# Scores of both query halves in one run of narrow products

## Chip, cores and metric

The kernel runs on one core of a Trainium2 chip. Its time is the device time of one execution in microseconds (us). The core has TensorE for matrix products (PE in profiles, its weight loads PEld), VectorE (DVE), ScalarE (ACT), GpSimd (POOL) and SyncE (SP), which issues the DMAs. Each engine works through its own queue in a fixed order; a semaphore makes an instruction wait for another engine. TensorE writes its sums into PSUM: eight banks, each of 128 rows by 512 float32 columns. VectorE and ScalarE read them from there.

## What is computed

Two layers of a decoder trunk over 256 positions of width 1024: a gated feed-forward half-step, a mixer, a second half-step and a gated embedding. Inside the mixer three branches run on one input projection `u @ w_in`. The change touches the first branch, in which an indexer chooses for each query the 64 keys that it may attend to:

```python
q_pos = j * Q_BLOCK + jnp.arange(Q_BLOCK)            # Q_BLOCK = 128: two halves
causal = key_pos[None, :] <= q_pos[:, None]
idx = jnp.einsum("bqh,bqhs->bqs", wi,
                 jax.nn.relu(jnp.einsum("bqhd,bsd->bqhs", qi, k_idx)))
idx = jnp.where(causal[None], idx.astype(jnp.float32), -jnp.inf)
_, sel = lax.top_k(idx, k_top)                       # k_top = 64
```

The other branches are a pooling mixer and a state-space mixer (SSD) with a causal depthwise convolution of width 4, `silu(causal_depthwise_conv(xbc, conv_w, conv_b))`, and a factor `silu(z)`.

## The kernel before

**Wide products.** Each float32 product is made of three products of rounded parts (`mm3`, L208 to L213): high by high, high by low, low by high. A column tile of a projection (128 output columns, 256 positions) is 24 such products of 128x256 over eight slices of the input. Weights come in units of 128x1024: SyncE loads `raw`, ScalarE rounds it to `whi` (L145), VectorE makes the remainder `wlo` (L146), with five buffers of each. One unit feeds 24 products.

**Banks.** All eight banks belong to one pool with two tags of four buffers (`bank`, L97): `mm` for wide products, two column tiles to a bank, and `aux` for everything else. A bank is taken again when its readers are done with it.

**The woven stage.** In the mixer three generators take turns by a plan of due times (`weave`): `choose` (key norms, transposes, then the indexer of the first and of the second half), `silus` (six pairs of column tiles for the convolution, four pairs of `z`, two of `q`) and `gates`. A pair of the convolution's input is read from its bank column tile by column tile: ScalarE scales it (L771), VectorE adds three shifted taps (L773, shapes 128x255, 128x254, 128x253), ScalarE takes the silu (L776). A gate pair is read by one tanh (L632), a `z` pair by one silu (L618).

**The indexer.** A narrow product multiplies 64 rows instead of 128; two of them, on the upper and the lower rows of the array, write two banks in turn (`products`). The first half of the queries sees 128 keys: 24 products of 64x128 into two `aux` banks. The second sees 256: 24 products of 64x256 into four `aux` banks. Then, for each half, ScalarE takes the Relu of each bank (L806), VectorE adds the eight heads with their weights (L811, L813; width 128 or 256), GpSimd masks future keys (L817), and VectorE takes eight rounds of the eight largest values: `max` (L824) and `match_replace` (L825), then a comparison and a product (L828, L829).

**What sets the order.** The code's order gives each instruction a place, narrow products keep theirs on TensorE (`mm`, `keep_in_program_order`), and when the program is built a scheduler, which simulates a timeline of its own, sets the order of each engine's queue. At run time that order is fixed.

Of the kernel before, what the change touches and what calls it, by code (L numbers as in the profile page):

```python
# [16 lines left out]
P = 128  # L17
# [51 lines left out]
class Builder:  # L69
# [440 lines left out]
    def mix(self, layer, nxt):  # L510
# [13 lines left out]
        idx = big2[:, 19:21]  # L524
        sm = self.a([P, 2, 96], F, "sm")[:, :, :88]
# [22 lines left out]
        qi = [self.a([P, 4, S], FR, "a4", 7) for _ in range(2)]  # L548
        for i in range(0, 4, 2):
            ps = self.in_pair(layer, T_QI + i, u0)  # L550
# [18 lines left out]
        q = [self.a([P, 4, S], FR, "a4", 7) for _ in range(2)]  # L569
        mb = [None, None]  # L570
        ki = [self.a([P, S], FR, "ki", 2) for _ in range(2)]
        ct = self.a([P, 2, 2, S], FR, "ct")

        def choose():
            v4 = self.t([P, 4], tag="v4", bufs=1)
            nc.vector.tensor_scalar(v4[:, :2], ss[:, :2], 1.0 / 256, EPS, op0=OP.mult, op1=OP.add)
            nc.vector.tensor_scalar(v4[:, 2:], ss[:, 2:], 1.0 / 64, EPS, op0=OP.mult, op1=OP.add)
            rk = self.t([P, 4], tag="rk", bufs=1)
            self.rsqrt(rk, v4, 4)
            for h in range(2):  # L580
                nc.vector.tensor_scalar(cn[:, h], cn[:, h], rk[:, h:h + 1], None, op0=OP.mult)
                nc.vector.tensor_scalar(ki2[:, h], sm[:, h, None, 8:72].to_broadcast([P, 2, 64]),
                                        rk[:, 2 + h:3 + h], None, op0=OP.mult)
            yield
            yield
            yield
            pk = self.bank("aux")
            for h in range(2):
                self.transpose(pk[:, h * P:(h + 1) * P],
                                    ki2[:, h].rearrange("p a b -> p (a b)"), self.ident)  # L590
            self.split_scaled(ki[0], ki[1], pk[:, :S], self.col(layer, "idx_k_norm"))
            yield
            yield
            pc = self.bank("aux")
            for c in range(2):
                for h in range(2):
                    self.transpose(pc[:, c * S + h * P:c * S + (h + 1) * P],
                                        cn[:, h, c * P:(c + 1) * P], self.ident)
            for c in range(2):
                self.split_scaled(ct[:, 0, c], ct[:, 1, c], pc[:, c * S:(c + 1) * S],  # L600
                                  self.col(layer, "kv_norm", c))
            yield
            mb[0] = yield from self.indexer(layer, 0, sm, qi, ki, idx[:, 0])
            mb[1] = yield from self.indexer(layer, 1, sm, qi, ki, idx[:, 1])

        def silus():
            for i in range(0, 12, 2):
# [29 lines left out]
        def some(n):  # L637
            for _ in range(n):
                next(gate)
                yield  # L640

        self.weave((choose(), 28, 1.08), (silus(), 60, 1), (some(12), 12, 1))


# [86 lines left out]
        for cs in ((0, 1), *((c,) for c in range(2, 8))):  # L731
            ps = [self.bank()[:, :S] for _ in cs]
# [49 lines left out]
        return ([g // 2 * 2 * n + 2 * j + odd for j in range(n)],  # L782
                slice(odd * 64, odd * 64 + 64))

    def products(self, g, per, qs, nk, q, key):


        sides = [(self.bank("aux"), *self.heads(g + i, per)) for i in range(2)]
        for j in range(per):
            for x, y in ((0, 0), (1, 0), (0, 1)):  # L790
                for ps, heads, rows in sides:
                    c = heads[j] // 2
                    self.mm(ps[:, j * nk:(j + 1) * nk], q[x][rows, c, qs],
                                          key(y, c)[rows, :nk], start=(x + y == 0), stop=(y == 1))
        return [(ps, heads) for ps, heads, _ in sides]

    def indexer(self, layer, h, sm, qi, ki, idx):

        nc = self.nc
        nk = (h + 1) * P  # L800
        per = 512 // nk
        qs = slice(h * P, (h + 1) * P)
        for ps, heads in [x for g in range(0, 8 // per, 2)
                          for x in self.products(g, per, qs, nk, qi, lambda y, c: ki[y])]:
            t = self.t([P, 512])
            nc.scalar.activation(t, ps, AF.Relu)  # L806
            for j, hd in enumerate(heads):
                w = sm[:, h, hd:hd + 1]
                tj = t[:, j * nk:(j + 1) * nk]
                if hd == 0:  # L810
                    nc.vector.tensor_scalar(idx[:, :nk], tj, w, None, op0=OP.mult)  # L811
                else:
                    nc.vector.scalar_tensor_tensor(idx[:, :nk], tj, w, idx[:, :nk],  # L813
                                                   op0=OP.mult, op1=OP.add)
            yield

        nc.gpsimd.affine_select(out=idx[:, h * P:nk], in_=idx[:, h * P:nk], pattern=[[-1, P]],  # L817
                                compare_op=OP.is_ge, fill=NEG, base=0, channel_multiplier=1)

        wk = self.a([P, S], F, "idxw", 2)  # L820
        m8 = self.t([P, 8], tag="m8", bufs=2)
        for i in range(8):
            cur = idx if i == 0 else wk
            nc.vector.max(m8, cur[:, :nk])  # L824
            nc.vector.match_replace(wk[:, :nk], m8, cur[:, :nk], NEG)  # L825
            yield

        nc.vector.tensor_tensor(wk[:, :nk], wk[:, :nk], idx[:, :nk], op=OP.is_equal)  # L828
        nc.vector.tensor_scalar(wk[:, :nk], wk[:, :nk], 1.0e30, None, op0=OP.mult)  # L829
        return wk  # L830
# [555 lines left out]
```

## Time and profile before

| | |
|---|---|
| median of 3 runs | 1311.74 us (1311.6 to 1311.91) |
| the profiled execution | 1311.92 us, its span 1310.0 us |
| TensorE busy | 1301.2 us, 99% of the span |
| VectorE busy | 1040.6 us, 79% |
| ScalarE busy | 741.1 us, 57% |
| granted clock, mean | 0.998 of 2.4 GHz |

The span runs from the first to the last instruction that the profiler saw; the execution's time is 1.9 us longer. A busy share is a mean over stages: VectorE has 79% in all and more in the mixer. A matmul's row shows the time until its end (some 0.28 us for 128x256), while the next one starts much earlier; so the spacing of starts is what a product costs.

### The profile page before, as it was taken

The numbers are of one execution on the slowest core, as the hardware profiler recorded it, in microseconds if no ns is written. First come the engines' busy times: TensorE is split into PE (matmuls) and PEld (weight loads), VectorE is DVE, ScalarE is ACT, GpSimd is POOL, SyncE is SP. The second block draws the span as 40 slices with busy tenths as digits, with TensorE's granted clock in tenths as the row PEclk, the third lists the DMA queues.
The fourth block names the chain that finished last, engine by engine and source line by source line (L and its number), as shares of the span: only waits on it lengthen the run. The fifth ranks groups of instructions, "written<-read, shape, count | busy, mean of one in ns | idle before, by whom it ended". The sixth has DMA issues, their size and how long they took to land.

```text
span 1310.0 us, 28317 instructions
## 1 busy us (share of the span) xinstructions
PE 1301.2 (99%) x11508; PEld 1293.0 (99%) x11508; DVE 1040.6 (79%) x1981; ACT 741.1 (57%) x1213; POOL 7.0 (1%) x17
## 2 busy tenths in 40 slices
PE   9999999999999999999999999999999999999997
PEld 8999999999999999999999999999999999999997
DVE  7877669988999877766887776799789988777667
ACT  6555446656874554444655554566577546544454
POOL 0000000000000000000000000000000000000000
PEclk9999999999999999999999999999999999999999
DMA  7655656565647566666556665556565566666561
GB/s 272 219 193 193 194 158 209 178 193 195 184 130 246 167 212 195 195 194 194 184 192 195 193 193 189 167 193 192 189 198 156 180 199 217 195 193 197 192 195 52
DMA packets 72242, 248.41 MB, mean 190 GB/s; under 512 B 7920, under 2 KB 10416, under 8 KB 72112
## 3 DMA queue, kind: packets, MB, share of 16 engines
q1 hardware_dynamic: 71680, 245.82, 58.0%
q8 instruction: 90, 1.47, 0.5%
q10 hardware_dynamic: 432, 0.79, 0.2%
q14 instruction: 40, 0.33, 0.1%
HBM read 245.50 MB, written 1.08 MB: 188 GB/s over the span
## 4 chain that ended last, share of the span: by engine, by line
PE 97%; DVE 1%; DMA 1%; ACT 0%; issue 0%; SPq 0%; DVEq 0%; ACTq 0%
PE mm L212 30%; PE mm L213 30%; PE mm L211 30%; PE aux L111 3%; PE aux L213 1%; PE aux L212 1%; PE aux L211 1%; PE aux L114 1%; DMA raw<-in_w_dram 1%; PE mm L111 0%; PE mm L496 0%; DVE wlo L146 0%; DVE acc L291 0%; ACT whi L145 0%; DVE rs_t L265 0%
## 5 line engine op out<-in xcount | busy, mean ns | idle before, releaser
L145 ACT CAST whi<-raw 128x1024 fp32r<-128x1024 f32 (+1 forms) x456 | 475.4, 1045 | 482.9 <-issue 221.3
L146 DVE TENSOR_TENSOR wlo<-raw,whi 128x1024 fp32r<-128x1024 f32 (+1 forms) x456 | 551.1, 1214 | 188.1 <-ACT whi L145 186.2
L213 PE MATMUL mm<-uh,wlo 128*128 128x256 f32 x2480 | 684.0, 277 | 0.3 <-DVE wlo L146 0.3
L212 PE MATMUL mm<-ul,whi 128*128 128x256 f32 x2480 | 683.4, 276 | 0.0
L211 PE MATMUL mm<-uh,whi 128*128 128x256 f32 x2441 | 673.0, 277 | 0.1
L213 PEld LDWEIGHTS mm<-uh,wlo 128*128 128x128 f32 x2480 | 465.1, 188 | 0.6 <-DVE wlo L146 0.5
L212 PEld LDWEIGHTS mm<-ul,whi 128*128 128x128 f32 x2480 | 465.3, 188 | 0.2 <-DVE ul L245 0.2
L211 PEld LDWEIGHTS mm<-uh,whi 128*128 128x128 f32 x2441 | 456.8, 188 | 0.8 <-ACT uh L244 0.3
L212 PE MATMUL mm<-gl,whi 128*128 128x256 f32 x704 | 194.1, 276 | 0.0
L213 PE MATMUL mm<-gh,wlo 128*128 128x256 f32 x704 | 194.1, 276 | 0.0
L211 PE MATMUL mm<-gh,whi 128*128 128x256 f32 x704 | 193.7, 276 | 0.0
L212 PEld LDWEIGHTS mm<-gl,whi 128*128 128x128 f32 x704 | 132.1, 188 | 0.0
L213 PEld LDWEIGHTS mm<-gh,wlo 128*128 128x128 f32 x704 | 132.1, 188 | 0.0
L211 PEld LDWEIGHTS mm<-gh,whi 128*128 128x128 f32 x704 | 131.8, 188 | 0.0
L212 PE MATMUL mm<-a,whi 128*128 128x256 f32 x256 | 70.7, 277 | 0.0
L211 PE MATMUL mm<-a,whi 128*128 128x256 f32 x256 | 70.6, 276 | 0.0
L213 PE MATMUL mm<-a,wlo 128*128 128x256 f32 x256 | 70.0, 276 | 0.0
L212 PEld LDWEIGHTS mm<-a,whi 128*128 128x128 f32 x256 | 48.1, 188 | 0.0
L211 PEld LDWEIGHTS mm<-a,whi 128*128 128x128 f32 x256 | 48.1, 188 | 0.0
L213 PEld LDWEIGHTS mm<-a,wlo 128*128 128x128 f32 x256 | 47.8, 188 | 0.0
L445 DVE TENSOR_TENSOR t<-mm,rs_r 128x256 f32<-128x256 f32 x88 | 37.2, 423 | 9.3 <-PE mm L213 0.6
L450 DVE SCALAR_TENSOR_TENSOR t<-t,t 128x256 f32<-128x256 f32 x88 | 37.4, 425 | 2.9
(280 smaller groups left out, 1224.2 us busy)
## 6 DMA issues: line engine op xcount, KB each, us to landing
raw<-in_w_dram SPq DMA_DIRECT2D x446, 512.0 KB, 4.3
gh<-rates SPq DMA_DIRECT2D x16, 256.0 KB, 4.2
raw<-in_w_dram SPq DMA_DIRECT2D x8, 352.0 KB, 3.1
a<-in_x_dram SPq DMA_DIRECT2D x3, 512.0 KB, 6.1
gh<-rates SPq DMA_DIRECT2D x8, 128.0 KB, 3.9
out_dram<-uh SPq DMA_DIRECT2D x3, 256.0 KB, 2.0
a<-in_x_dram SPq DMA_DIRECT2D x1, 544.0 KB, 3.6
raw<-in_w_dram SPq DMA_DIRECT2D x2, 256.0 KB, 3.2
```

Source lines behind the costliest of these rows:

```text
L111: self.tc.keep_in_program_order(self.nc.tensor.matmul(*args, **kw))
L114: self.tc.keep_in_program_order(self.nc.tensor.transpose(*args))
L145: nc.scalar.copy(hi[:, :n], raw[:, :n])
L146: ins = nc.vector.tensor_tensor(lo[:, :n], raw[:, :n], hi[:, :n].bitcast(F), op=OP.subtract)
L211: (self.mm if keep else mm)(ps, a[0], b[0], start=start, stop=False)
L212: mm(ps, a[0], b[1], start=False, stop=False)
L213: mm(ps, a[1], b[0], start=False, stop=stop)
L445: nc.vector.tensor_tensor(t, p1[0], r, op=OP.mult)
L450: nc.vector.scalar_tensor_tensor(g, th, 1.0, t, op0=OP.add, op1=OP.mult)
```

## The change

`index_scores` issues the products of both halves one after the other, before either half's Relu, sums and top-k. The first half's scores go to two banks of the `mm` tag, since the second half's fill all four of `aux`. `indexer` keeps the rest and takes the banks as an argument.

```diff
-            mb[0] = yield from self.indexer(layer, 0, sm, qi, ki, idx[:, 0])
-            mb[1] = yield from self.indexer(layer, 1, sm, qi, ki, idx[:, 1])
+            scores = [self.index_scores(h, qi, ki) for h in range(2)]
+            for h in range(2):
+                mb[h] = yield from self.indexer(layer, h, sm, scores[h], idx[:, h])
...
-    def products(self, g, per, qs, nk, q, key):
-        sides = [(self.bank("aux"), *self.heads(g + i, per)) for i in range(2)]
+    def products(self, g, per, qs, nk, q, key, tag="aux"):
+        sides = [(self.bank(tag), *self.heads(g + i, per)) for i in range(2)]
...
+    def index_scores(self, h, qi, ki):
+        nk = (h + 1) * P
+        per = 512 // nk
+        return [x for g in range(0, 8 // per, 2)
+                for x in self.products(g, per, slice(h * P, (h + 1) * P), nk, qi,
+                                       lambda y, c: ki[y], "aux" if h else "mm")]
```

On TensorE, in layer 0, the first narrow run stood before in the middle of the pair `mm_3009` (an input of the convolution); `mm_2819` is a gate pair, `mm_3132` the next input of the convolution. The second narrow run, into `aux_3455` to `aux_3470`, came 240 rows later.

```order
L213 MATMUL mm_3009<-uh_2738,wlo_2852 128x256
L111 MATMUL aux_3040<-ki_2775,a_377_2606 128x128 [waits Activation_49]
L111 MATMUL aux_3041<-ki_2775,a_377_2606 128x128
...
L111 MATMUL aux_3041<-ki_2776,a_377_2606 128x128
L211 MATMUL mm_3009<-uh_2738,whi_2906 128x256
...
L213 MATMUL mm_2819<-uh_2738,wlo_2822 128x256
L211 MATMUL mm_3132<-uh_2738,whi_2941 128x256 [waits DVE_49,Activation_49]
```

Now there is one run on TensorE, 36 wide products later, behind the end of the gate pair; `mm_3160` is what `mm_3132` was. Further down, 240 wide products behind the run, `mm_3522` is the second pair of `z` (the first, `mm_3450`, starts 60 products before it).

```order
L213 MATMUL mm_2819<-uh_2738,wlo_2822 128x256
L111 MATMUL mm_3040<-ki_2775,a_377_2606 128x128 [waits DVE_49,Activation_49]
L111 MATMUL mm_3041<-ki_2775,a_377_2606 128x128 [waits Activation_49]
...
L111 MATMUL mm_3041<-ki_2776,a_377_2606 128x128
L111 MATMUL aux_3066<-ki_2775,a_377_2606 128x256
...
L111 MATMUL aux_3081<-ki_2776,a_377_2606 128x256
L211 MATMUL mm_3160<-uh_2738,whi_2941 128x256 [waits DVE_49,Activation_49]
...
L213 MATMUL mm_3276<-uh_2738,wlo_3279 128x256
L211 MATMUL mm_3522<-uh_2738,whi_3387 128x256 [waits DVE_49,Activation_49]
```

The first two narrow products now carry waits for VectorE and ScalarE, which the ones into `aux` did not.

On ScalarE, at the same place, stood before the Relu of the two banks (L806), two silus, and further down the tanh of the gate pair `mm_2819`.

```order
L806 ACTIVATE t_448_3066<-aux_3040 128x512 [waits PE_49]
L806 ACTIVATE t_453_3120<-aux_3041 128x512 [waits PE_49]
L776 ACTIVATE gh_2487<-t_427_2886,cc_90 128x256 [waits DVE_49,Activation_49]
L776 ACTIVATE gh_2487<-t_436_2970,cc_90 128x256 [waits DVE_49,Activation_49]
L771 ACTIVATE t_440_2994<-mm_2904,cc_90 128x256
L145 CAST whi_3073<-raw_3072 128x1024 [waits DMAHW1_49,PE_49]
L771 ACTIVATE t_452_3114<-mm_3009,cc_90 128x256 [waits PE_49]
L145 CAST whi_3134<-raw_3133 128x1024 [waits DMAHW2_49,PE_49]
L632 ACTIVATE gh_2487<-mm_2819 128x512 [waits PE_49]
```

Now ScalarE has two weight casts and one silu ahead of that tanh (L634 in the new numbering), and the Relu (L812) of the same two banks behind it.

```order
L145 CAST whi_3101<-raw_3100 128x1024 [waits DMAHW1_49,PE_49,Activation_49]
L778 ACTIVATE gh_2487<-t_427_2886,cc_90 128x256 [waits DVE_49,Activation_49]
L145 CAST whi_3162<-raw_3161 128x1024 [waits DMAHW2_49,PE_49]
L634 ACTIVATE gh_2487<-mm_2819 128x512 [waits PE_49]
L778 ACTIVATE gh_2487<-t_436_2970,cc_90 128x256 [waits DVE_49,Activation_49]
L773 ACTIVATE t_440_2994<-mm_2904,cc_90 128x256
L773 ACTIVATE t_456_3142<-mm_3009,cc_90 128x256
L812 ACTIVATE t_452_3094<-mm_3040 128x512 [waits PE_49]
L812 ACTIVATE t_457_3148<-mm_3041 128x512 [waits PE_49]
```

The tanh moved ahead of the Relu, and the casts and the silu ahead of the tanh.

On VectorE, where the taps end that free the bank for the second pair of `z`, stood before the last rounds of the first half's top-k (width 128) and nothing of the second half; the freeing tap is the row of `t_478_3307` of width 253.

```order
L824 MAX m_460_3155<-idxw_3154 128x8 [waits DVE_49]
L773 SCALAR_TENSOR_TENSOR t_478_3307<-mm_3217,cc_90,t_478_3307 128x255 [waits Activation_49]
L773 SCALAR_TENSOR_TENSOR t_486_3390<-mm_3313,cc_90,t_486_3390 128x255 [waits Activation_49]
L825 MATCH_REPLACE idxw_3154<-m_460_3155,idxw_3154 128x128 [waits DVE_49]
L773 SCALAR_TENSOR_TENSOR t_478_3307<-mm_3217,cc_90,t_478_3307 128x254 [waits DVE_49]
L773 SCALAR_TENSOR_TENSOR t_486_3390<-mm_3313,cc_90,t_486_3390 128x254 [waits DVE_49]
L828 TENSOR_TENSOR idxw_3154<-idxw_3154,gl_2488 128x128 [waits DVE_49]
L773 SCALAR_TENSOR_TENSOR t_478_3307<-mm_3217,cc_90,t_478_3307 128x253 [waits DVE_49]
```

Now the second half's last rounds (width 256, L830 and L831 in the new numbering) stand on VectorE between those taps, and two weight remainders; the freeing tap is the last row, on `mm_3245`.

```order
L146 TENSOR_TENSOR wlo_3428<-raw_3426,whi_3427 128x1024 [waits DMAHW1_49,PE_49,Activation_49]
L830 MAX m_521_3658<-idxw_3657 128x8 [waits DVE_49]
L775 SCALAR_TENSOR_TENSOR t_482_3335<-mm_3245,cc_90,t_482_3335 128x255 [waits Activation_49]
L775 SCALAR_TENSOR_TENSOR t_490_3418<-mm_3341,cc_90,t_490_3418 128x255 [waits Activation_49]
L831 MATCH_REPLACE idxw_3657<-m_521_3658,idxw_3657 128x256 [waits DVE_49]
L775 SCALAR_TENSOR_TENSOR t_482_3335<-mm_3245,cc_90,t_482_3335 128x254 [waits DVE_49]
L775 SCALAR_TENSOR_TENSOR t_490_3418<-mm_3341,cc_90,t_490_3418 128x254 [waits DVE_49]
L834 TENSOR_TENSOR idxw_3657<-idxw_3657,gl_2488 128x256 [waits DVE_49]
L146 TENSOR_TENSOR wlo_3453<-raw_3451,whi_3452 128x1024 [waits DMAHW2_49,PE_49,Activation_49]
L775 SCALAR_TENSOR_TENSOR t_482_3335<-mm_3245,cc_90,t_482_3335 128x253 [waits DVE_49]
```

All sixteen sums and nearly the whole of both halves' top-k moved ahead of this tap.

## Rows read from the trace of the kernel before

**Rows 1.** The page: span, and shares of the chain that ended last.

```profile
span 1310.0 us, 28317 instructions
...
PE 97%; DVE 1%; DMA 1%; ACT 0%; issue 0%; SPq 0%; DVEq 0%; ACTq 0%
```

**Rows 2.** Windows: us, busy time of each engine (instructions), clock, DMA share, GB/s.

```profile
225.00:267.00 42.00, 42.00 (x390) 41.54 (x389) 40.61 (x97) 29.75 (x50) 2.37 (x2) 1.00 0.58 187
```

**Rows 3.** Timeline of TensorE around both narrow runs: start, us, instruction.

```profile
225.31 0.28 PE L213 MATMUL mm<-uh,wlo 128*128 128x256 f32 x1
225.51 1.55 PE L111 MATMUL aux<-ki,a 64*128 64x128 f32 x24
227.00 0.39 PE L211 MATMUL mm<-uh,whi 128*128 128x256 f32 x1
227.22 0.28 PE L212 MATMUL mm<-ul,whi 128*128 128x256 f32 x1
...
254.20 0.28 PE L213 MATMUL mm<-uh,wlo 128*128 128x256 f32 x1
254.41 1.70 PE L111 MATMUL aux<-ki,a 64*128 64x256 f32 x24
256.03 0.39 PE L211 MATMUL mm<-uh,whi 128*128 128x256 f32 x1
```

**Rows 4.** VectorE's groups, 225 to 275: count | busy us, mean ns | idle before.

```profile
L146 DVE TENSOR_TENSOR wlo<-raw,whi 128x1024 fp32r<-128x1024 f32 x17 | 20.6, 1214 | 0.0
L773 DVE SCALAR_TENSOR_TENSOR t<-mm,cc,t 128x253 f32<-128x253 f32 x11 | 5.0, 473 | 0.0
...
L813 DVE SCALAR_TENSOR_TENSOR gl<-t,sm,gl 128x256 f32<-128x256 f32 x7 | 3.4, 480 | 0.1
L824 DVE MAX8 m<-idxw 128x8 f32<-128x256 f32 x6 | 2.6, 426 | 0.1
L813 DVE SCALAR_TENSOR_TENSOR gl<-t,sm,gl 128x128 f32<-128x128 f32 x7 | 2.4, 346 | 0.1
L825 DVE MATCH_REPLACE8 idxw<-m,idxw 128x256 f32<-128x256 f32 x5 | 2.0, 409 | 0.0
L824 DVE MAX8 m<-idxw 128x8 f32<-128x128 f32 x7 | 2.0, 290 | 0.1
L825 DVE MATCH_REPLACE8 idxw<-m,idxw 128x128 f32<-128x128 f32 x7 | 1.9, 276 | 0.0
```

**Rows 5.** Timeline of VectorE: first weighted sum, direct successors, taps, spacing.

```profile
229.90 0.28 DVE L811 TENSOR_SCALAR gl<-t,sm 128x128 f32<-128x128 f32 x1
230.22 0.74 DVE L813 SCALAR_TENSOR_TENSOR gl<-t,sm,gl 128x128 f32<-128x128 f32 x2
...
255.46 0.86 DVE L773 SCALAR_TENSOR_TENSOR t<-mm,cc,t 128x253 f32<-128x253 f32 x2
...
258.32 0.48 DVE L773 SCALAR_TENSOR_TENSOR t<-mm,cc,t 128x255 f32<-128x255 f32 x1
258.72 0.47 DVE L813 SCALAR_TENSOR_TENSOR gl<-t,sm,gl 128x256 f32<-128x256 f32 x1
```

**Rows 6.** GpSimd's masks (ns min/median/max), and VectorE's maximum behind one, with its idle time.

```profile
L817 POOL TENSOR_SCALAR_AFFINE_SELECT gl<-gl x4: 1132/1186/1216, 236.7 to 910.1; 128x128 f32<-128x128 f32 x4
...
264.66 0.43 DVE L824 MAX8 m<-gl 128x8 f32<-128x256 f32 x1 [0.18 <-POOL gl L817]
```

**Rows 7.** Timeline of ScalarE from the first silu to the tanh.

```profile
229.30 0.51 ACT L776 ACTIVATE gh<-t,cc 128x256 f32<-128x256 f32 x1 [0.66 <-DVE t L773]
...
230.85 1.04 ACT L145 CAST whi<-raw 128x1024 fp32r<-128x1024 f32 x1
...
233.10 0.60 ACT L632 ACTIVATE gh<-mm 128x512 f32<-128x512 f32 x1
```

**Rows 8.** Windows at the program's end: columns as in rows 2.

```profile
1302.30:1305.40 3.10, 0.75 (x5) 0.28 (x3) 2.68 (x17) 1.96 (x5) 0.00 (x0) 1.00 0.14 54
1305.40:1306.50 1.10, 0.00 (x0) 0.00 (x0) 0.72 (x2) 0.69 (x1) 0.00 (x0) 0.56 0.87 326
```

More of the change, by code (lines that the diff above doesn't have):

```diff
@@ L795, in products, with indexer @@
         return [(ps, heads) for ps, heads, _ in sides]
-    def indexer(self, layer, h, sm, qi, ki, idx):
+    def index_scores(self, h, qi, ki):
[4 more added lines that the diff above has]
+                                       lambda y, c: ki[y], "aux" if h else "mm")]
+    def indexer(self, layer, h, sm, scores, idx):
         nc = self.nc
         nk = (h + 1) * P
[L801 to L804, printed above, removed]
+        for ps, heads in scores:
             t = self.t([P, 512])
```

## Prediction

> **What bounds the kernel now.** Read the page first: span and chain. The span is 1310.0 us, and 97% of the chain that ended last is TensorE [rows 1]. So TensorE is never out of work for long, and an edit helps only if it shortens TensorE's own queue, and hurts by every microsecond that it makes this queue wait. Next, the stretch in which the indexer works, by engine: in 225 to 267 us TensorE is busy for all of its 42.00 us, but VectorE is busy for 40.61 of them, ScalarE for 29.75 [rows 2]. VectorE has 1.4 us in hand in 42. Third, TensorE's timeline around the two narrow runs [rows 3]: what a switch costs, and how far apart wide products start. Last, VectorE's groups and timeline [rows 4, 5], to see how long its queue takes if its order changes.
>
> **What the change takes away: one switch in each layer.** A narrow run stands between wide products. The last wide one before it starts at 225.31 and the first narrow one at 225.51: 0.20 where wide products follow each other at 0.1134 (227.22 to 254.20 is 238 of them) [rows 3]. The 24 narrow products take 1.49 to the first wide one (0.062 each on average, though the last step is again a switch of some 0.20), and the second wide one starts 0.22 later. A run taken away saves 0.09 at its start, 0.14 at its end and 0.11 after that: 0.34 us. The first half's run (1.49) and the second's (256.03 less 254.41, 1.62) then cost 3.17 with the switch into them, 0.20. Products, shapes and counts stay as they are; DMA issues and GpSimd's queue keep their order. Gain: 0.34 x 2 layers = 0.7 us.
>
> **What it adds: waits for banks.** The wide pool has four banks. By the new order the two banks of the first half's scores are those in which mm_2800 and mm_2819 stood, and the pair that the scores push on, mm_3160, gets the one of mm_2904. Four things follow; I work them out in layer 0, on the clock of the trace of before.
>
> *Wait A.* The second narrow product waits for ScalarE's tanh of mm_2819, which TensorE now finishes just ahead of it. TensorE gets there at 225.31 + 36 wide products x 0.1134 + 0.20 = 229.6. ScalarE does the silu that in the trace starts at 229.30 when VectorE's tap ends, one weight cast and then the tanh: 229.30 + 0.51 + 1.04 + 0.60 less two overlaps of 0.09 = 231.3 [rows 7]. Wait: 1.7 us. All narrow products, and 240 wide ones, are queued behind it.
>
> *Waits C and D.* VectorE must do the three taps of a convolution on each column tile before a bank comes free. The first z pair, mm_3450, takes the bank of mm_3160, the second, mm_3522, that of mm_3245, and the order puts the second half's weighted sums and its whole top-k ahead of those taps, where before they stood behind. What decides is the last of these taps, on mm_3245. Ahead of it and with it stand, from the first row that moved: 10 weight remainders, 23 taps, 8 weighted sums of width 128 and 8 of width 256, and for each width 8 maxima and 8 replacements (counted in the order). VectorE's independent instructions start some 0.08 before the one ahead of them ends (258.32 to 258.72 for a row of 0.48) [rows 5]; so from the means in [rows 4] the steps are 1.13 for a remainder (11.3 us), 0.39 for a tap (9.0), 0.40 for a 256 sum (2.95, the first being short), 0.35 and 0.21 for the maxima (2.8 and 1.7), 0.41 and 0.28 for the replacements with their loads (3.3 and 2.2). Of the 128 sums five follow each other directly, at 0.37 as in the row of two that takes 0.74, the rest at 0.27: 2.6. Two comparisons and a product: 0.7. Sum 36.55 us.
>
> Beside this VectorE now waits for GpSimd. Its mask takes 1.13 to 1.22 us, and already in the trace a maximum waited 0.18 for it with two long rows between [rows 6]. In the new order one 256 sum (0.40) stands between the first mask's sum and its maximum, and 0.5 of short rows before the second's: 0.8 + 0.7 = 1.5 us of idle VectorE.
>
> VectorE's first such row starts at 229.90 [rows 5], so the deciding tap ends at 229.90 + 36.55 + 1.5 + 0.08 = 268.0. TensorE, were it free of all these waits, would reach mm_3522 at: last wide before the run 229.39, run 3.17, the slow step 0.22, and 239 steps of 0.1134 = 27.1, that is 259.9. It is 8.1 us late. A, C and D are parts of this one lateness, not added to it: 1.7 at A; the 16 rows between the last taps of mm_3160 and mm_3245 are 9.1 us, so the first ends at 258.9, where TensorE wants its bank at 254.8 (with A's delay): C is 4.1; the rest, 2.3, is D. The wait at mm_3160 itself I put within 0.2.
>
> A second way to the same number: in the trace the tap that frees the bank for mm_3522 ends at 256.32 (two taps from 255.46, 0.86) [rows 5], and TensorE takes that bank 24 wide products after 256.03, at 258.9: 2.5 us in hand. The change puts 8 sums, 8 maxima, 8 replacements and a comparison of width 256 ahead (9.4 us), one more remainder (1.1) and 1.5 of mask, and TensorE has 12 more wide products (1.4) to do less the 0.34: 12.0 less 2.5 less 1.1 is 8.4. I take 8.1, the longer sum's.
>
> ScalarE's six Relu now come at once; it has 12 us idle of 42 [rows 2], so only their place ahead of the taps' first steps counts, and that is behind VectorE anyway. What was behind the second top-k is now early, but nothing of it bounded TensorE, so it gives nothing back. Sum for a layer: 8.1 less 0.34 = 7.8; both layers stand alike, 15.6 us. Against the profiled execution: 1311.92 + 15.6 = 1327.5; the median of the runs is 0.2 lower, 1311.74, so 1327.3. Bounds: without the masks' idle time 6.6 a layer, 1324.3; if no VectorE rows overlapped, 83 x 0.08 = 6.6 more a layer, 1340. The steps are read off this very stretch, so I stay near them.
>
> The Trainium skill, TensorEngine Tiling (Array Packing), section PSUM Bottleneck, speaks against the change in general: small tiles speed up TensorE, not the emptying of PSUM. The trace agrees as far as it goes: 3.1 us of narrow products leave 16 sums that cost VectorE 5.5.
>
> **Rivals.** *Not slower.* VectorE's queue could be through with the taps in time: place, the tap on mm_3245; price, nothing but the switch; it decides if that tap ends by 259.9. Then 1311.74 - 0.7 = 1311.1, no change that could be told. For it: no wait of this kind shows in the chain of before. Against it: 40.61 of 42 us busy [rows 2], and 8.1 us are missing. 0.06.
>
> *Only wait A.* VectorE's rows might pass so much faster that four banks cover C and D: 1311.74 + 2 x (1.7 - 0.34) = 1314.5. It needs the top-k to cost half of its rows. 0.09.
>
> *The clock falls.* C leaves TensorE idle for some 4 us. In the trace the granted clock stays 1.00 (2.4 GHz) through a stretch in which TensorE is busy for 0.75 of 3.10 us, and the next stretch has it at 0.56 on average, after the last product [rows 8]. If it drops to 1.2 GHz in C, the 60 wide products up to D take up to 6.8 us more; D hides 2.3 of that, so between 0 and 4.5 a layer, 1327.3 to 1336.3; I take the middle, 1332. 0.10. The Trainium skill, TensorE: Matmul & The Clock Gate, section A second HAM failure mode: psum-queue depth-cycling, says that short idle times between groups that cycle through PSUM banks can make the clock swing; by that rule this rival would be the forecast. The row of 3.10 us shows one such idle time without it, so I leave it a rival.
>
> **How the numbers follow.** Forecast 0.75, with its own range 1322 to 1332; clock 0.10; only A 0.09; not slower 0.06. The range that leaves out not more than 2 in 10 goes from 1319 to 1334. A measurement of this kernel tells 0.2% (2.6 us) from no change: faster 0.02, within 0.2% 0.07 (the not slower case, and a little of the A case, which stands at 0.21%), slower 0.91.
>
> **What would show it.** In the profile after: one narrow run a layer, 48 products, with some 1.7 us before its second product; TensorE idle by some 4 us at some 30 us behind the run and 2.3 us seven later, both ended by VectorE's tap; VectorE without an idle time there but for two of 0.7 to 0.8 us ended by GpSimd. TensorE's idle time of the whole span grows by 16 us. The forecast is wrong if these waits are missing or end on another engine, or if VectorE takes its sums and top-k at other steps than here.

## The result, and the profile after

The changed kernel takes 1326.45 us (median; 1324.41 to 1327.85), the kernel before, run beside it, 1311.83 (1311.6 to 1311.99): a ratio of 1.0114, 95% interval 1.0101 to 1.0126. The prediction said 1327.3. The profiled execution took 1327.85, its span 15.6 us more than that in [rows 1]. Here is its page: the span, the engines' busy times, and the shares of the chain that ended last.

```profile
span 1325.6 us, 28329 instructions
...
PE 1308.2 (99%) x11508; PEld 1299.9 (98%) x11508; DVE 1038.0 (78%) x1981; ACT 741.1 (56%) x1213; POOL 3.6 (0%) x17
...
PE 87%; DVE 8%; ACT 2%; issue 2%; DMA 1%; POOL 0%; DVEq 0%; ACTq 0%; POOLq 0%
```

VectorE, 1% of the chain before, now has 8% of it. What TensorE waits for (line, releaser: us in total, times, longest) names the places:

```profile
PE mm L211 <- DVE t L775: 6.1, 4, 2.0
PE mm L111 <- ACT gh L634: 3.1, 2, 1.6
```

Six waits, three in each layer. Neither row was there before. TensorE's timeline in layer 0 shows them one by one, to be held against [rows 3]:

```profile
228.68 0.28 PE L213 MATMUL mm<-uh,wlo 128*128 128x256 f32 x1
228.89 0.32 PE L111 MATMUL mm<-ki,a 64*128 64x128 f32 x1
230.79 1.55 PE L111 MATMUL mm<-ki,a 64*128 64x128 f32 x23 [1.58 <-ACT gh L634]
232.08 2.56 PE L111 MATMUL aux<-ki,a 64*128 64x256 f32 x24
234.56 0.58 PE L211 MATMUL mm<-uh,whi 128*128 128x256 f32 x1
234.94 0.41 PE L212 MATMUL mm<-ul,whi 128*128 128x256 f32 x1
...
257.02 0.36 PE L211 MATMUL mm<-uh,whi 128*128 128x256 f32 x1 [1.03 <-DVE t L775]
...
266.07 0.36 PE L211 MATMUL mm<-uh,whi 128*128 128x256 f32 x1 [1.99 <-DVE t L775]
...
266.86 0.41 PE L211 MATMUL mm<-uh,whi 128*128 128x256 f32 x1
267.07 0.41 PE L212 MATMUL mm<-ul,whi 128*128 128x256 f32 x1
```

There is one run of 48 narrow products; its second one waits 1.58 us for the tanh (A), the first `z` pair 1.03 us for a tap (C), the second 1.99 us for another (D). From 234.56 and from 266.86 on the wide products are 0.21 apart instead of 0.113: that is the clock. Windows of the same stretch (us, busy time of each engine, granted clock, DMA share, GB/s; the second was 42.00 us of TensorE before, [rows 2]):

```profile
225.00:232.00 7.00, 5.42 (x58) 5.15 (x57) 6.46 (x11) 6.30 (x12) 0.00 (x0) 1.00 0.62 208
225.00:267.00 42.00, 37.39 (x330) 36.57 (x330) 41.03 (x113) 24.77 (x42) 0.71 (x2) 0.96 0.45 149
232.70:236.10 3.40, 3.40 (x26) 3.18 (x23) 3.19 (x10) 2.96 (x8) 0.00 (x0) 0.50 0.71 239
257.00:266.80 9.80, 7.79 (x66) 7.64 (x67) 9.80 (x22) 5.93 (x10) 0.00 (x0) 1.00 0.66 212
266.90:270.20 3.30, 3.30 (x17) 3.30 (x17) 2.84 (x5) 1.81 (x4) 0.00 (x0) 0.50 0.80 267
270.30:276.00 5.70, 5.70 (x52) 5.70 (x52) 2.85 (x3) 3.00 (x4) 0.00 (x0) 1.00 0.57 198
```

Behind A and behind D the clock goes to 1.2 GHz (0.50) for 3.4 us and comes back; below this is called a fall. Layer 1 does the same, as two windows within its falls show:

```profile
888.20:891.40 3.20, 3.20 (x22) 2.98 (x20) 2.99 (x10) 2.76 (x7) 0.00 (x0) 0.50 0.63 209
922.30:925.50 3.20, 3.20 (x17) 3.20 (x17) 2.57 (x5) 1.55 (x4) 0.00 (x0) 0.50 0.80 265
```

3.4 us at half speed are 1.7 us of work lost, with TensorE busy all the while, so that no column of idle time shows it. The sum over the span closes roughly: idle 6.1 + 3.1, four falls of 1.7, less two switches of 0.34, make 15.3 of the 15.6 us. It leaves out two terms of opposite sign. A wait costs some 0.2 to 0.3 us more than its idle time, because a product's row runs on after the next one could start: 228.89 to 230.79 is 1.90, for 1.58 of idle, where narrow products otherwise follow each other at some 0.06. And this execution came to 228.68 some 0.7 us ahead of the 229.39 that the trace of before gives; where it gained them stays open.

### The profile page after: what moved, and what is told of

It reads as the page before. It is cut to its first block, busy times and chain, and to the rows that moved or that the text cites. A ratio compares the mean times of both kernels' runs of the same rounds, so it can differ in the third digit from the quotient of the medians.

```text
span 1325.6 us, 28329 instructions
## 1 busy us (share of the span) xinstructions
PE 1308.2 (99%) x11508; PEld 1299.9 (98%) x11508; DVE 1038.0 (78%) x1981; ACT 741.1 (56%) x1213; POOL 3.6 (0%) x17
## 4 chain that ended last, share of the span: by engine, by line
PE 87%; DVE 8%; ACT 2%; issue 2%; DMA 1%; POOL 0%; DVEq 0%; ACTq 0%; POOLq 0%
PE mm L212 27%; PE mm L213 27%; PE mm L211 26%; DVE wlo L146 2%; PE aux L111 2%; DVE t L775 1%; PE aux L212 1%; PE aux L213 1%; PE aux L211 1%; PE mm L221 1%; DVE m L830 1%; DVE idxw L831 1%; DMA raw<-in_w_dram 1%; ACT whi L145 1%; PE aux L114 1%
```

## The experiments

The question that they settle: is the loss VectorE's queue, put in a worse order (theory 1, that of the prediction), or the two banks taken from the wide products, whatever VectorE does (theory 2)? And what is the clock's part?

**e1, VectorE's order put back.** A token (`turn`), which the weight remainders carry too, keeps the second half's first weighted sum behind the remainders issued ahead of it in the code. Banks and the narrow run are as changed.

```diff
-                    nc.vector.tensor_scalar(idx[:, :nk], tj, w, None, op0=OP.mult)
+                    ins = nc.vector.tensor_scalar(idx[:, :nk], tj, w, None, op0=OP.mult)
+                    if h:
+                        self.turn(ins)
```

> The changed kernel, but the second half's weighted sums and top-k are kept behind the weight remainders and taps that the code issues before them, so that VectorE has them about where it had them before the change; one run of narrow products and its banks stay as changed (a wide pair's first 12 products also move 24 places forward). Theory 1 (what costs is VectorE's queue: the sums and the top-k stand ahead of the taps that free the banks): the two waits on taps, 1.03 and 1.99 us a layer, vanish; the wait on the tanh, 1.6 us, stays, and 0.34 is saved: 1311.8 + 2 x (1.6 - 0.34) = 1314.3. If the clock falls behind that wait as in the changed kernel, up to 1.6 a layer comes on top, since no later wait hides it now: 1314 to 1317.5. Theory 2 (what costs is that two banks of the wide pool are taken): the waits stay, 1324 to 1328.

Measured 1317.58 us (1314.45 to 1318.01; ratio 1.0040, 1.0027 to 1.0054): 8.9 less than the changed kernel. C and D are gone. TensorE's timeline and a window behind the wait:

```profile
229.86 0.32 PE L111 MATMUL mm<-ki,a 64*128 64x128 f32 x1
231.48 1.55 PE L111 MATMUL mm<-ki,a 64*128 64x128 f32 x23 [1.29 <-ACT gh L634]
```

```profile
233.30:236.60 3.30, 3.30 (x27) 3.08 (x24) 3.09 (x10) 2.86 (x7) 0.00 (x0) 0.52 0.73 257
```

Only A is left, and the clock falls behind it in each layer. The four runs took 1314.45, 1317.29, 1317.87 and 1318.01: the first lies on the sum without a fall (1314.3), with a mean clock of 0.999, the others, at 0.996, some 3.3 above it, which is two falls. So C and D come from VectorE's order, and a fall that no later wait hides costs its full 1.7.

**e2, only the banks.** The kernel before, two narrow runs, with the first half's scores in the wide pool (`products` takes the tag as in the change).

```diff
...
-                          for x in self.products(g, per, qs, nk, qi, lambda y, c: ki[y])]:
+                          for x in self.products(g, per, qs, nk, qi, lambda y, c: ki[y],
+                                                 "aux" if h else "mm")]:
```

> The kernel before, two narrow runs and its order of the indexer's work, but with the first half's scores in two banks of the wide products' pool; nothing is merged. Theory 1 (VectorE's queue): taking the banks costs the wait on the tanh, some 1.6 us a layer, and at most as much again at the wide pair behind it, whose bank the same engines free; no wait some 30 us later: 1311.8 + 2 x 1.6 = 1315.0, up to 1318.5 with a second wait or a fall of the clock. Theory 2 (banks): as slow as the changed kernel, 1324 to 1328.

Measured 1323.03 (1322.4 to 1323.84; ratio 1.0087, 1.0074 to 1.0101). Neither theory had this time. Timeline and window:

```profile
230.87 1.55 PE L111 MATMUL mm<-ki,a 64*128 64x128 f32 x23 [1.44 <-ACT gh L632]
233.93 0.55 PE L211 MATMUL mm<-uh,whi 128*128 128x256 f32 x1 [1.51 <-DVE t L773]
```

```profile
233.40:240.00 6.60, 6.07 (x28) 6.10 (x29) 5.27 (x17) 2.60 (x6) 0.29 (x1) 0.50 0.28 89
888.70:891.90 3.20, 3.20 (x17) 3.20 (x16) 2.85 (x9) 0.57 (x2) 0.05 (x1) 0.50 0.24 96
```

Both waits that theory 1 allowed are there, 2.9 us a layer, and no wait 30 us later; so the banks alone do not make C and D. But they are not cheap: the clock stays at half for 6.6 us in layer 0 and for some 3.4 in layer 1, which I had counted once at most. 2 x 2.9 and some 5 for the clock make 10.8 of the 11.5 that the two banks cost here with nothing else changed. In the changed kernel TensorE shows no wait at the second of these places; the second half's narrow products, 1.6 us at full clock, now stand ahead of it.

**e3, less work on VectorE, and e10, its control.** One round of top-k for the second half, in the changed kernel and in the kernel before.

```diff
         for i in range(8):
+            if h and i:
+                yield
+                continue
```

> The changed kernel with one round instead of eight in the second half's top-k; seven rounds of a maximum and a replacement are left out, so its selection is not the reference's. Theory 1 (VectorE's queue): a round of width 256 takes 0.35 + 0.41 us from start to start, seven take 5.3 us off the queue ahead of the deciding tap; of the lateness of 6.9 us a layer only the wait on the tanh is left, 1.6 us: 1311.8 + 2 x (1.6 - 0.34) = 1314.3, up to 1317.5 where the clock falls behind that wait. Theory 2 (banks): the top-k touches no bank, so no change, 1324 to 1328.

> The control to the third experiment: the kernel before with one round instead of eight in the second half's top-k; seven rounds are left out. Theory 1 (there VectorE's queue never made TensorE wait): no change, 1311.0 to 1312.0, so what the third experiment won was won from the new waits alone. Theory 2 (less work on VectorE is worth time in either kernel): 2 us or more under the kernel before.

e3 took 1315.57 (1313.81 to 1317.31; ratio 1.0031, 1.0021 to 1.0040), e10 1311.43 beside 1311.23 of before (ratio 0.9999, 0.9990 to 1.0008). Seven rounds less are worth 10.9 us in the changed kernel and nothing in the one before. In e3's profiled execution, one of 1314.35 with a mean clock of 0.999, only A is left, and the clock did not fall behind it:

```profile
231.14 1.55 PE L111 MATMUL mm<-ki,a 64*128 64x128 f32 x23 [1.30 <-ACT gh L634]
```

```profile
231.40:240.00 8.60, 8.58 (x98) 8.40 (x96) 8.20 (x23) 6.41 (x14) 0.41 (x1) 1.00 0.38 127
```

The same wait, 1.3 us, is followed by a fall in e1 and by none here. This goes with the times: e3's nine runs lie 3.5 us apart, the three fastest at a mean clock of 0.999 and the slowest, 1317.31, at 0.996.

**e5, e6 and e7, waits filled with products that nobody reads.** They keep a wait's time and take away TensorE's idleness. e5 is e1, e6 is e2 and e7 is the changed kernel with

```diff
+    def fill(self, n):
+        if self.pre is None:
+            self.pre = self.bank("aux")
+        for _ in range(n):
+            self.mm(self.pre[:, :S], self.onesr,
+                    self.onesr[:, None, :].to_broadcast([P, 2, P]), start=True, stop=True)
...
                     self.mm(ps[:, j * nk:(j + 1) * nk], q[x][rows, c, qs],
                                           key(y, c)[rows, :nk], start=(x + y == 0), stop=(y == 1))
+                    if tag == "mm" and ps is sides[0][0] and j == x == y == 0:
+                        self.fill(12)
```

e6 has 13 such products more behind the last product of the first narrow run.

> The first experiment with TensorE's wait on the tanh filled: behind the first narrow product 12 products of 128x256 on constants, into a bank that is free, 12 x 0.113 = 1.36 us; nobody reads them. Theory 1 (the runs of the first experiment at 1317.3 to 1318.0 beside one at 1314.45 differ by two falls of the clock of 1.7 us, and TensorE's idle time brings them): the time lost to the wait stays, 1.4 a layer, the clock does not fall: every run between 1313.9 and 1315.0. Theory 2 (the falls come from the narrow products or by chance, not from the idle time): single runs up to 1318 remain, median 1316 to 1318.

> The second experiment (two runs, the first half's scores in two wide banks) with both its waits filled in the same way: 12 products on constants behind the first narrow product, 13 behind the last one of that run. Theory 1 (idle time brings the falls): two waits of 1.4 and 1.5 us a layer stay as lost time and three falls of the clock go: 1311.5 + 2 x 2.9 = 1317.3, between 1316.5 and 1318.5. Theory 2 (the falls have another reason): 1322 to 1324 as before.

> The changed kernel with only its first wait filled, 12 products on constants behind the first narrow product of each layer. Theory 1 (the taps on VectorE set the end of that stretch, and the fall of the clock behind the first wait was hidden in the wait on the first of them): without that fall TensorE comes some 1.6 us earlier to the first tap's wait, which grows from 1.03 to 2.6 us; the next stays near 2.0; the time does not gain from it, 1324 to 1328, with falls behind those waits. Theory 2 (every fall costs its 1.6 us): 3.2 less than the changed kernel, 1323.2 at most, and the wait on the first tap stays at 1.0.

e5 took 1314.33, and its eleven runs lie between 1313.93 and 1315.0 (ratio 1.0021, 1.0012 to 1.0031): 3.3 less than e1 for 24 products more. e6 took 1318.48 (1317.87 to 1319.52; ratio 1.0054, 1.0041 to 1.0068), 4.6 less than e2 for 50 products more; it stands 1.2 above the sum, of which the switches into and out of the fillers can be a part. Timeline of e5, then the same window of e5 and of e6:

```profile
229.72 1.69 PE L111 MATMUL aux<-onesr 128*128 128x256 f32 x12
231.34 1.55 PE L111 MATMUL mm<-ki,a 64*128 64x128 f32 x23
```

```profile
231.40:240.00 8.60, 8.60 (x98) 8.47 (x98) 7.83 (x24) 6.10 (x14) 0.29 (x1) 1.00 0.39 126
```

```profile
231.90:240.00 8.10, 8.10 (x82) 8.03 (x82) 7.36 (x22) 4.59 (x10) 0.29 (x1) 1.00 0.41 135
```

The clock is 1.00 in both. None of e5's eleven runs and of e6's four has a mean clock under 0.998, where three of e1's four had 0.996. That TensorE's idle time brings the falls, though not each time, is so shown for these waits.

e7 took 1325.53 (1324.19 to 1326.27; ratio 1.0106, 1.0092 to 1.0120). The next waits of its timeline, in layer 0 and layer 1:

```profile
256.86 0.36 PE L211 MATMUL mm<-uh,whi 128*128 128x256 f32 x1 [2.47 <-DVE t L775]
...
265.90 0.35 PE L211 MATMUL mm<-uh,whi 128*128 128x256 f32 x1 [0.33 <-DVE t L775]
...
910.45 0.36 PE L211 MATMUL mm<-uh,whi 128*128 128x256 f32 x1 [2.52 <-DVE t L775]
919.50 0.36 PE L211 MATMUL mm<-uh,whi 128*128 128x256 f32 x1 [1.96 <-DVE t L775]
```

C grew from 1.03 to 2.47 and ended at the same moment, 256.86 for 257.02. So the fall behind A had eaten 1.5 us of C and cost nothing by itself: VectorE's tap sets the end. In layer 0 of this execution the clock fell behind C instead, which ate most of D (0.33 for 1.99), and no fall came behind D:

```profile
257.60:260.90 3.30, 3.30 (x17) 3.30 (x17) 3.30 (x8) 1.37 (x3) 0.00 (x0) 0.50 0.65 206
```

The median is 0.9 below the changed kernel's, which is within the noise (the two intervals overlap).

**e8, the masks by themselves.**

```diff
-        nc.gpsimd.affine_select(out=self.up, in_=self.ones, pattern=[[-1, P]],
-                                compare_op=OP.is_gt, fill=0.0, base=0, channel_multiplier=1)
+        for _ in range(150):
+            nc.gpsimd.affine_select(out=self.up, in_=self.ones, pattern=[[-1, P]],
+                                    compare_op=OP.is_gt, fill=0.0, base=0, channel_multiplier=1)
```

> The kernel before with GpSimd writing one constant tile (128x128, by the instruction of the masks) 150 times in place of once, at the start, beside the feed-forward's work on VectorE. Theory 1 (a mask that meets a weight remainder of VectorE, 1.22 us, waits for its end): two kinds of masks, 0.3 to 0.4 us where no remainder runs, and 0.5 to 1.6 us where one does. Theory 2 (the 1.13 to 1.22 us of the masks in the kernel before are the price of a mask after a long idle time, or of a mask in place): all but the first take 0.3 to 0.4 us, whatever VectorE does.

Theory 1 holds (the kernel took 1312.91 us). All of them as a group (ns min/median/max), then two of the timeline, GpSimd's and VectorE's:

```profile
L359 POOL TENSOR_SCALAR_AFFINE_SELECT up<-ones x150: 290/357/1362, 1.6 to 88.9; 128x128 f32<-128x128 f32 x150
```

```profile
30.34 1.16 POOL L359 TENSOR_SCALAR_AFFINE_SELECT up<-ones 128x128 f32<-128x128 f32 x1
```

```profile
30.04 1.30 DVE L146 TENSOR_TENSOR wlo<-raw,whi 128x1024 fp32r<-128x1024 f32 x1 [0.68 <-ACT whi L145]
```

The mask that starts within the remainder ends at 31.50, behind it (31.34), and takes 1.16. 31 of the 150 masks start within a remainder: they take 1.16 to 1.36, median 1.16, and each ends 0.15 or 0.16 behind that remainder. Of the 119 others the median is 0.30 and the longest 0.63. The remainder pays too: the median of the 31 remainders from 3 to 89 us is 1.30, of those in the kernel before 1.22.

**e4 and e9, a version without the waits.** e1 with more turns of the indexer's generator ahead of the scores, four in e4, five in e9, so that the run stands a pair of column tiles later, when the tanh is done.

```diff
+            for _ in range(5):
+                yield
             scores = [self.index_scores(h, qi, ki) for h in range(2)]
...
-        self.weave((choose(), 28, 1.08), (silus(), 60, 1), (some(12), 12, 1))
+        self.weave((choose(), 33, 1.08), (silus(), 60, 1), (some(12), 12, 1))
```

> The first experiment, with four more turns of the indexer's generator ahead of the scores: the run of narrow products comes some 48 wide products (5.4 us) later. Theory 1: by then the tanh is done (it ends 1.6 us after TensorE wants it in the changed kernel), so the wait on it vanishes too, TensorE does not idle and the clock does not fall; what is left is the saved switch: 1311.8 - 0.7 = 1311.1, between 1310.8 and 1312.5, that is no difference that a reader need care for, but about 15 us under the changed kernel. Theory 2 (banks, wherever the run stands): 1314 or more.

> The fourth experiment with five turns instead of four ahead of the scores. There the first narrow product stood 12 wide products ahead of the other 47, which is a second switch; here all 48 stand together in both layers. Theory 1 (a switch saved is 0.34 us a layer, and nothing waits): the stretch from the last wide product before the run to the second behind it takes 0.20 + 3.05 + 0.22, some 0.3 a layer less than the two pieces of the fourth experiment; a wait of 0 to 0.3 us on the bank freed last may be left: 1310.8 to 1311.5, at best 0.7 under the kernel before, which is under what a measurement can tell. Theory 2 (a joint run saves no switch): 1312.1 as there.

e4 took 1312.12 (1311.63 to 1312.87; ratio 1.0004, 0.9995 to 1.0013), with TensorE busy for 41.92 of the 42 us:

```profile
225.00:267.00 42.00, 41.92 (x387) 41.39 (x387) 38.94 (x90) 29.44 (x50) 0.29 (x1) 1.00 0.56 184
```

No wait, no fall, but no gain either: one narrow product stands alone, 12 wide ones ahead of its run, which is a second switch and would give the saving back. In e9 all stand together. Its timeline:

```profile
235.18 0.28 PE L213 MATMUL mm<-uh,wlo 128*128 128x256 f32 x1
235.38 0.32 PE L111 MATMUL mm<-ki,a 64*128 64x128 f32 x1
235.91 1.53 PE L111 MATMUL mm<-ki,a 64*128 64x128 f32 x23 [0.20 <-DVE t L777]
237.19 1.71 PE L111 MATMUL aux<-ki,a 64*128 64x256 f32 x24
238.83 0.39 PE L211 MATMUL mm<-uh,whi 128*128 128x256 f32 x1
239.06 0.28 PE L212 MATMUL mm<-ul,whi 128*128 128x256 f32 x1
```

1311.15 beside 1311.23 (ratio 0.9999, 0.9990 to 1.0008): the change's idea with its waits taken out is as fast as the kernel before, and no faster that could be told. The second narrow product comes 0.53 behind the first, a small wait that is left for a bank. From the last wide product before the run (235.18) to the second behind it (239.06) it takes 3.88, where the forecast's terms make 3.39 (3.17 + 0.22): the 0.5 lost there is more than the 0.34 of a switch. No version that beats both kernels was found.

## Why the prediction was right, and where it was wrong

*The mechanism was right.* The lateness is VectorE's queue, in the order that the change gives it: put back (e1) or shortened (e3), C and D go, and what is filled ahead of them (e7) is given back at them. Two rows of VectorE's timeline after, the first that moved and the freeing taps:

```profile
229.41 2.35 DVE L146 TENSOR_TENSOR wlo<-raw,whi 128x1024 fp32r<-128x1024 f32 x2
...
265.44 0.87 DVE L775 SCALAR_TENSOR_TENSOR t<-mm,cc,t 128x253 f32<-128x253 f32 x2
```

The first of the two last taps, the one on `mm_3245`, ends near 265.9, some 36.5 us behind 229.41, where the sum of means said 36.55. The steps read off [rows 4, 5] held in another order. At this tap TensorE was 6.9 us late, where 8.1 were forecast: it starts again at 266.07, and the forecast's own steps from 228.68 (3.17, 0.22 and 27.1) would have had it there at 259.2.

*The switch* is not shown by itself: no version here has a joint run without a wait in it, and in e9 the wait costs more than the 0.34.

*Wait A*: 1.7 forecast, 1.58 and 1.49 measured.

*The masks failed.* The step "0.8 + 0.7 = 1.5 us of idle VectorE" a layer measured 0.18. GpSimd's two masks after, and the one maximum that waited:

```profile
238.66 0.41 POOL L823 TENSOR_SCALAR_AFFINE_SELECT gl<-gl 128x128 f32<-128x128 f32 x1 [235.78 <-DVE gl L819]
242.34 0.29 POOL L823 TENSOR_SCALAR_AFFINE_SELECT gl<-gl 128x128 f32<-128x128 f32 x1 [3.27 <-DVE gl L819]
```

```profile
239.10 0.29 DVE L830 MAX8 m<-gl 128x8 f32<-128x128 f32 x1 [0.18 <-POOL gl L823]
```

I took the 1.13 to 1.22 us of [rows 6] for the price of a mask. They are the price of a mask that starts within a weight remainder, as e8 shows; the new order has none there. In the kernel before, VectorE's remainder and GpSimd's mask ahead of the maximum in [rows 6] were:

```profile
263.25 1.22 DVE L146 TENSOR_TENSOR wlo<-raw,whi 128x1024 fp32r<-128x1024 f32 x1
```

```profile
263.41 1.22 POOL L817 TENSOR_SCALAR_AFFINE_SELECT gl<-gl 128x128 f32<-128x128 f32 x1 [25.51 <-DVE gl L813]
```

Only one row, this remainder, stood between the mask's sum and the maximum, not the two that the prediction read there. The Trainium skill, SBUF — State Buffer, section Who interferes with whom, says that a VectorE instruction with two inputs in SBUF contends with a GpSimd instruction that reads SBUF, and that such contention is an exclusive lock; the trace agrees, with 1.16 for 0.30.

*C* was forecast at 4.1 and is 2.5 where no fall of the clock stands ahead of it (e7): 1.3 of the difference is the masks'. In the changed kernel it is 1.03, the rest being lost at half clock instead. *D* was forecast at 2.3 and is 1.99.

*The clock*, a rival with 0.10, took part in all runs of the changed kernel (mean clock 0.993 to 0.996, before 0.998), but otherwise than I priced it: in the profiled execution behind A and D, which I had not looked at, and not in C. The one behind A is hidden in C, the one behind D costs 1.6 to 1.7 a layer. The stretch in [rows 8] on which I played the rival down shows one idle time without a fall, and one such row decides little: e1 and e3 show the same wait with and without. The Trainium skill, TensorE: Matmul & The Clock Gate, section A second HAM failure mode: psum-queue depth-cycling, was nearer. It tells of frequent short idle times between groups that cycle through PSUM banks; here a single wait for a bank, 1.29 us in e1, was enough, though not each time.

*So the sum was right by two errors that cancel*, and that is luck: 1.3 a layer too much for the masks, 1.6 too little for the clock. The forecast's own lower bound, "without the masks' idle time 6.6 a layer, 1324.3", is what the mechanism gives where no fall behind D costs anything. The fastest run of the changed kernel took 1324.41, at a mean clock of 0.996 where the slowest had 0.993; that its falls were only the hidden ones behind A fits this, but is not shown. Likewise "TensorE's idle time of the whole span grows by 16 us" was wrong: by the busy times it grew by 8.6 us (17.4 of 1325.6 for 8.8 of 1310.0), and the other 7.0 are longer busy time, most of it at half clock. What stays open is what decides, at the same wait, whether the clock falls.

## What to carry to other kernels

When two engines are both near full, as here, work moved ahead on the off-path engine can be paid on the path where it next waits for a buffer: look for what else stands in that queue, above all for reads that free a PSUM bank. A wait of 1.3 to 2.0 us on TensorE in an else dense stretch can cost twice, once idle and once at half clock; the busy column doesn't show the second part, the spacing of the products and the granted clock do. Before a duration from a trace is used in a new order, look at what ran beside it there.

## What the runs showed of the hardware

- The granted clock fell to 1.2 GHz behind waits of 1.3 to 2.5 us of a TensorE that had been at 2.4 GHz and busy, mostly for 3.4 us, once for 6.6. It did not fall each time: e1 and e3 had the same wait of 1.3 with and without, and a wait of 1.03 in the changed kernel had none behind it. Products that nobody reads, put into the wait, prevented it (e5, e6).
- Runs of one kernel differ with these falls: 3.5 us between the fastest and the slowest of e1 (mean clock 0.999 and 0.996), 1.1 in e5, whose runs all have 0.998 or 0.999.
- A GpSimd mask of 0.30 us takes 1.16 or more when it starts within a VectorE remainder of 1.22 us, and ends 0.15 behind it; the remainder takes 1.30 beside masks (e8).
